# Splitting the second stream's blocks of normed tiles in halves of 512 columns

## The chip, the cores and the metric

One core of a Trainium2 chip runs the whole program: a two-layer network on 256 latent and 256 context tokens, in float32. The metric is the device time of one execution in microseconds (us). Engines are named as in the profile: PE is TensorE (matmul), DVE VectorE, ACT ScalarE, POOL GpSimd, SP SyncE; the last three also start DMAs.

## The reference, cut to what matters

```python
def _modulate(t, g, shift, scale):
    return _rms(t, g) * (1 + scale) + shift

def _swiglu(h, w13, w2):
    gte, up = jnp.split(h @ w13, 2, axis=-1)
    return (jax.nn.silu(gte) * up) @ w2

def _short_conv_mixer(h, w_in, k, w_out):
    bgate, cgate, xv = jnp.split(h @ w_in, 3, axis=-1)
    return (bgate * _dwconv3(cgate * xv, k)) @ w_out

# layer 0: FFN, conv mixer, FFN; layer 1: FFN, attention mixer, FFN; lat and cx are the two streams
lat = lat + 0.5 * mod[:, 0, 2] * _swiglu(_modulate(lat, norm_g[i, 0], ...), ffn_w13[i, 0], ffn_w2[i, 0])
cx = cx + 0.5 * modc[0, 2] * _swiglu(_modulate(cx, norm_g[i, 0], ...), ffn_w13[i, 0], ffn_w2[i, 0])
h = _modulate(lat, norm_g[i, 1], mod[:, 1, 0], mod[:, 1, 1])
hc = _modulate(cx, norm_g[i, 1], modc[1, 0], modc[1, 1])
...
```

The model width is 1024, the hidden width 2816. Every stage begins with the norm of the residual (RMS, scale, shift) of both streams, and then multiplies the normed tiles by that stage's first weights.

## The kernel before, in words

The residual `x` lies transposed, features on partitions: eight k tiles of 128 features, each 512 columns wide, columns 0 to 255 for the latent stream (s = 0) and 256 to 511 for the context stream (s = 1).

**Precision.** Each float32 operand is split in a rounded part and the rest (`split`: ACT copies the rounded part, L107; DVE subtracts it, L108). A product is then three matmuls (`mm3`): high by high (L136), the moving operand's low part (L137), the weights' low part (L138). So a matmul on L136 needs ACT's result alone, and one on L137 needs DVE's subtraction too. Names ending in h and l are such parts: `bh`, `bl` of the normed tiles, `wh`, `wl` of weights, `th`, `tl` of block sums.

**Blocks.** In three stages (the conv mixer, the second FFN of layer 0, the first FFN of layer 1) the normed tiles are kept as four blocks of 128 x 1024: features 0 to 511 or 512 to 1023, of stream 0 or 1. Each block holds four k tiles of 256 columns, as a float32 tile `hr` and as `bh`, `bl`. `Blocks.block` makes them: for each k tile, DVE scales x by the norm (`scaled`, L299, tile `t`, three buffers) and ACT adds the shift (L396, into `hr`). For stream 0 (`fine`) the two parts are made tile by tile (L391, L392). For stream 1 they are made once the four tiles of the block are there, by one `split` of 1024 columns.

**Openings.** The first work of such a stage is `opening`. PE multiplies two weight tiles by both streams, stream 0 first: 8 k tiles x 2 outputs (`pg`, `pu`) x 3 matmuls of 256 columns, for each weight tile. Under the second weight tile's products of stream 0 the norm of stream 1 is computed (`turn` in `tail_norm`), and then PE turns to stream 1. Meanwhile DVE and ACT build the sums of blocks T1 to T4 from the `hr` tiles (`sums`, L417 to L424).

**Pairs.** All further weights go through `Pair`, seven products of blocks in place of eight: `head` (A11 and A12), `five` (S1 by T1), `six` (S2 by T2, S4 by a block), `seven` (S3 by T3) and `four` (A22 by T4), accumulating in the PSUM tiles `p` and `q`. DVE forms the weights' sums (L731, L739), ACT and DVE split them, and DVE adds the halves of `q` and `sg` (L768).

**What sets the order.** Outside a few stretches that are ordered by hand, a scheduler places each engine's instructions in a queue, from its own estimate of when their inputs are there; each queue then runs in that order. So the code's order and the queue's differ, and a change of size moves instructions around it. Where a queue's next instruction waits, all behind it wait.

The function `tick(n)` places n pieces of the modulation vectors' work (DVE, L177) at its place in the code.

Of the kernel before, what the change touches and what calls it, by code (L numbers as in the profile page):

```python
# [20 lines left out]
T2 = 2 * S  # L21
# [27 lines left out]
def hybrid_kernel(ctx: ExitStack, tc: tile.TileContext, a: dict, out: bass.AP):  # L49
# [17 lines left out]
    def psum(s="ps"):  # L67
        return psm.tile([P, T2], F32, tag="mm", name=nm(s))
# [37 lines left out]
    def split(hi, lo, src):  # L106
        nc.scalar.activation(out=hi, in_=src, func=AF.Copy)  # L107
        return nc.vector.tensor_tensor(out=lo, in0=src, in1=hi.bitcast(F32), op=ALU.subtract)  # L108
# [80 lines left out]
    def streams(l, ch):  # L189
        return 1 if l == 1 and ch >= 5 else 2  # L190
# [9 lines left out]
    def next_unit():  # L200
        if not units:
            l, ch, pair, j = jobs.pop(0)
            mod_tile(l, ch)
            raw = coming.pop() if coming else load_mod(l, ch, pair, j)
            if jobs:
                coming.append(load_mod(*jobs[0]))
            units.extend((l, ch, pair, raw, j, v) for v in range(streams(l, ch)))
        if place:
            with tc.issue_after(place[0]):
                mod_unit(*units.pop(0))  # L210
        else:
            mod_unit(*units.pop(0))

    def tick(n, at=None):

        place[:] = [at] if at else []
        owed[0] += n
        while (jobs or units) and owed[0] >= 1:
            owed[0] -= 1
            next_unit()  # L220
        place.clear()
# [17 lines left out]
    def gate_of(l, j):  # L239

        ch = 3 * j + 2

        def get(m):
            while done.get((l, ch), 0) < (m // 2 + 1) * 2 * streams(l, ch):
                next_unit()
            return modv[l, ch]

        return get
# [66 lines left out]
    def hot(s, dt=F32R):  # L315
        return hop.tile([P, 1024], dt, name=nm(s), tag="hop")
# [56 lines left out]
    class Blocks:  # L373
# [5 lines left out]
        def block(self, s, hf, A, B, ri, fine=False, ks=range(4)):  # L379
            if ks[0] == 0:  # L380
                self.raw[hf, s] = hot("hr", F32)
                self.t["B", hf, s] = hot("bh"), hot("bl")
            raw = self.raw[hf, s]
            hi, lo = self.t["B", hf, s]
            for i in ks:
                k = 4 * hf + i
                c = slice(i * S, i * S + S)
                t = scaled(s, k, A, ri)
                b = B[:, k, s : s + 1]
                if fine:  # L390
                    nc.scalar.activation(out=hi[:, c], in_=t, func=AF.Identity, bias=b)  # L391
                    nc.vector.scalar_tensor_tensor(  # L392
                        out=lo[:, c], in0=t, scalar=b, in1=hi[:, c].bitcast(F32),
                        op0=ALU.add, op1=ALU.subtract,
                    )
                nc.scalar.activation(out=raw[:, c], in_=t, func=AF.Identity, bias=b)  # L396
            if not fine:
                split(hi, lo, raw)

        def at(self, k, c0, c1):  # L400
            return self.blk(("B", k // 4, c0 // S), k % 4)
# [411 lines left out]
    def ffn(l, b, h, tot, gate, tail, gs=(), ev=(0, 0), z=None):  # L813
        gs = list(gs)
        i0 = 0
        for t, n in enumerate(THIRDS):
            between = ()
            if tot == T2:
                heads = []
                if t == 0 and not gs:  # L820

                    gs = [new_pair("g") for _ in range(2)]
                    heads.append(opening(
                        h, [a["w13"][l, b, 0], a["w13"][l, b, 1], lambda: Pair(a["w13"][l, b, 2], h)],
                        lambda pp, i: w13_post(pp, gs[i], 0, T2),
                    ))
                prev = None
                for i in range(len(gs), n):
                    if t == 0 and not heads and i in AS_IS[l, b]:
                        w = load_w(a["w13"][l, b, i])  # L830
                        pp = psum("pg"), psum("pu")
                        if prev:
                            prev.seven()
                        if "T1" not in h.t:
                            with tc.issue_after(rows["W1"]):
                                h.sums()
                        w13_mm(pp, w, h, range(4), 0, T2)
                        if prev:
                            gs.append(new_pair("g"))
                            prev.four(gs[-1])  # L840
                            prev = None
                        w13_mm(pp, w, h, range(4, KT), 0, T2)
                        gs.append(new_pair("g"))
                        tick(3, w13_post(pp, gs[-1], 0, T2))
                        continue
                    if heads:
                        pr = heads.pop(0)
                    else:
                        pr = Pair(a["w13"][l, b, i0 + i], h)
                        pr.sums(0)  # L850
                        pr.sums(1)
                        pr.head()
                    pr.five()
                    at = prev.seven().ins if prev else None
                    pr.six()
                    if prev:
                        gs.append(new_pair("g"))
                        prev.four(gs[-1])
                    prev = pr
                    if i:  # L860
                        tick(0.9, at)

                def last():
                    gs.append(new_pair("g"))
                    prev.four(gs[-1])

                between = (prev.seven, last) if prev else ()
            else:
                for i in range(n):
                    w = load_w(a["w13"][l, b, i0 + i])  # L870
                    gs.append(beside(gp.tile([P, T2], F32R, name=nm("gx"), tag="gh")))
                    pp = psum("pg"), psum("pu")
                    if i0 + i < EARLY:
                        for k in range(KT):
                            for j in range(2):
                                ps = pp[j][:, : z.w]
                                mm3(ps, w(at13(1 - j, k)), z.at(k), k == 0, k == KT - 1)
                            if i == 0 and k == KT // 2:
                                flush(1)
                        if i < 3:  # L880
                            flush(1)
                        early_post(pp, gs[i], z.ri)
                        tick(1)
                        continue
                    for j in range(2):
                        ws = [w(at13(1 - j, k)) for k in range(KT)]
                        mm_wide(pp[j], ws, [h.both(k) for k in range(KT)], True, True)
                    beside_post(pp, gs[i])
                    tick(1)
            i0 += n  # L890

            def ws2(m):
                src = a["w2a"][l, b, m // 2] if t == 0 else a["w2b"][l, b, t - 1, m // 2]
                o = (m % 2) * n * P
                raw = load_raw(src[:, o : o + n * P], n * P)
                hi, lo = half()
                split(hi[:, : n * P], lo[:, : n * P], raw[:, : n * P])
                return lambda k: (hi[:, k * P : k * P + P], lo[:, k * P : k * P + P])

            cur = gs  # L900
            end = t == len(THIRDS) - 1
            project(
                ws2,
                (lambda k, c0, c1: cur[k]) if tot == S
                else lambda k, c0, c1: (cur[k][0][:, c0:c1], cur[k][1][:, c0:c1]), n,
                gate, tail if end else None, tot, 2 if end and tot == T2 else 0, ev[end], between,
            )
            gs = []


    h = Plain()
# [170 lines left out]
    ws, gs0, raws, cut = {}, [], {}, {}  # L1082
# [58 lines left out]
    h = FirstBlocks(h, h32)  # L1141
# [14 lines left out]


    hn = Blocks()
    ffn(0, 0, h, T2, gate_of(0, 0), tail_norm(0, 1, hn), gs0, (4, 3.4))
    h = hn  # L1160

    zs, ds = [], {}
# [52 lines left out]
    for n in range(2, len(parts)):  # L1215
# [8 lines left out]
        at = prev.seven().ins if prev else None  # L1224
# [22 lines left out]
    hn = Blocks()  # L1247
# [3 lines left out]
    )  # L1251
    h = hn
    hn = Blocks()
    ffn(0, 1, h, T2, gate_of(0, 2), tail_norm(1, 0, hn), (), (3.6, 3))
    h = hn


    hn = Plain()
    ffn(1, 0, h, T2, gate_of(1, 0), tail_norm(1, 1, hn), (), (2.8, 2.2))
    h = hn  # L1260
    ap = ctx.enter_context(tc.tile_pool(name="ap", bufs=2))

# [210 lines left out]
    aos, at, wos = [], [], {}  # L1473
    pieces = []
    for i in range(2):
        raw = [load_raw(a["wo"][i, :, c : c + 1024]) for c in (0, 1024)]
        hs = [half() for _ in range(2)]
        wos[i] = lambda o, hs=hs: tuple(t[:, o % 1024 : o % 1024 + P] for t in hs[o // 1024])
        for j in range(4):
            c = j % 2 * T2  # L1480
# [39 lines left out]
    hn, hz = Beside(), Early()  # L1520
# [89 lines left out]
```

## Time and profile before

| | |
|---|---|
| median of 3 runs | 1549.41 us (1548.96 to 1549.91) |
| the profiled execution | 1548.97 us, span 1547.2 us (1.8 us lie around the span) |
| granted TensorE clock | 1.00 |
| PE busy | 1533.5 us, 99% of the span |
| DVE, ACT, POOL busy | 1298.2, 852.2, 301.3 us |

A row of the timeline gives start and duration in us, engine, line, operation, output and inputs, shapes, count, and in brackets how long the engine was idle before it and what released it. Back-to-back instructions overlap in it, so what one costs its queue is the distance from its start to the next start. A matmul's end is modelled; how dense PE runs is read from starts. Line numbers are those of the kernel before; in the changed kernel all lines behind the edit stand one further.

### The profile page before, as it was taken

The page shows a single profiled execution, that of the slowest core. Times are in us where ns is not written, and L with a number is a line of the kernel's source. Part 1 is how long each engine was busy: PE and PEld are TensorE (multiplying, and loading weights), DVE is VectorE, ACT ScalarE, POOL GpSimd, SP SyncE. Part 2 cuts the span into 40 slices and gives each one's busy share as a digit, 9 for nine tenths or more (in the row PEclk, how much of TensorE's full clock was granted, in tenths as well). Part 3 has the DMA queues.
Part 4 walks back from the last instruction along what each step waited for, and adds up shares of the span by engine and source line. Part 5 has one row for each costly group of instructions (what it writes and reads, how often), then busy time and mean ns, then how long its engine had stood idle before and what let it go on. Part 6 is the DMA issues. An engine that isn't in the chain of part 4 may idle for free.

```text
span 1547.2 us, 27333 instructions
## 1 busy us (share of the span) xinstructions
PE 1533.5 (99%) x10594; PEld 1423.6 (92%) x10594; DVE 1298.2 (84%) x1964; ACT 852.2 (55%) x1468; POOL 301.3 (19%) x265
## 2 busy tenths in 40 slices
PE   8999999999999999999999999999999999999999
PEld 6898998999999899989999899989999899998888
DVE  5888788898989999968979889958968788998676
ACT  5644554645655376446456466446456456774553
POOL 0013313402231023042052112043042002300000
PEclk9999999999999999999999999999999999999999
DMA  9568768765356636695796625785697743476562
GB/s 377 199 188 235 162 184 232 164 194 143 75 143 175 206 91 151 212 216 135 213 214 153 207 68 136 220 189 138 210 220 182 253 159 114 142 246 220 170 195 76
DMA packets 97474, 278.80 MB, mean 180 GB/s; under 512 B 11456, under 2 KB 13120, under 8 KB 97344
## 3 DMA queue, kind: packets, MB, share of 16 engines
q1 hardware_dynamic: 69408, 228.10, 45.4%
q0 software_dynamic: 25920, 47.20, 18.1%
q10 hardware_dynamic: 2016, 1.76, 0.4%
q8 instruction: 83, 1.36, 0.4%
q14 instruction: 47, 0.39, 0.1%
HBM read 262.07 MB, written 1.05 MB: 170 GB/s over the span
## 4 chain that ended last, share of the span: by engine, by line
PE 89%; DVE 6%; DMA 2%; ACT 1%; issue 1%; POOL 0%; SPq 0%; DVEq 0%; POOLq 0%; ACTq 0%
PE p L138 8%; PE p L137 8%; PE p L136 8%; PE py L137 8%; PE py L136 8%; PE py L138 8%; PE q L138 6%; PE q L136 6%; PE q L137 6%; PE py L144 2%; PE pu L144 2%; PE pg L144 2%; DVE wl L108 1%; DMA wr<-in_w 1%; PE py L146 1%
## 5 line engine op out<-in xcount | busy, mean ns | idle before, releaser
L107 ACT ACTIVATE wh<-wr 128x1024 fp32r<-128x1024 f32 (+2 forms) x454 | 400.5, 909 | 289.2 <-PE py L137 94.5
L108 DVE TENSOR_TENSOR wl<-wr,wh 128x1024 fp32r<-128x1024 f32 (+2 forms) x454 | 468.6, 1056 | 107.0 <-ACT wh L107 87.0
L177 DVE CUSTOM_DVE_ANT_0 junk<-wr,scbc,first 128x1024 bf16<-128x1024 f32 x209 | 269.9, 1291 | 2.2 <-DMA wr<-in_modT 0.2
L137 PE MATMUL py<-gl,wh 128*128 128x512 f32 (+1 forms) x570 | 213.4, 374 | 0.0
L136 PE MATMUL py<-gh,wh 128*128 128x512 f32 (+1 forms) x570 | 213.4, 374 | 0.0
L138 PE MATMUL py<-gh,wl 128*128 128x512 f32 (+1 forms) x570 | 212.8, 373 | 0.0
L709 POOL TENSOR_SCALAR wr<-wr 128x512 f32<-128x512 f32 x66 | 125.4, 1900 | 424.0 <-DMA wr<-in_w 162.7
L136 PE MATMUL p<-th,wh 128*128 128x256 f32 x528 | 149.5, 283 | 0.0
L138 PE MATMUL p<-th,wl 128*128 128x256 f32 x528 | 149.4, 283 | 0.0
L137 PE MATMUL p<-tl,wh 128*128 128x256 f32 x528 | 149.4, 283 | 0.0
L138 PEld LDWEIGHTS py<-gh,wl 128*128 128x128 f32 x570 | 107.3, 188 | 19.1
L136 PEld LDWEIGHTS py<-gh,wh 128*128 128x128 f32 x570 | 107.4, 188 | 18.3
L137 PEld LDWEIGHTS py<-gl,wh 128*128 128x128 f32 x570 | 107.4, 188 | 18.2
L138 PE MATMUL q<-bh,wl 128*128 128x256 f32 x400 | 113.2, 283 | 0.0
L137 PE MATMUL q<-bl,wh 128*128 128x256 f32 x400 | 113.2, 283 | 0.0
L136 PE MATMUL q<-bh,wh 128*128 128x256 f32 x400 | 113.2, 283 | 0.0
L136 PEld LDWEIGHTS p<-th,wh 128*128 128x128 f32 x528 | 101.3, 192 | 0.4
L137 PEld LDWEIGHTS p<-tl,wh 128*128 128x128 f32 x528 | 101.3, 192 | 0.4
L138 PEld LDWEIGHTS p<-th,wl 128*128 128x128 f32 x528 | 101.3, 192 | 0.0
L114 POOL DMA_DIRECT2D w4l<-in_w x56 | 53.2, 949 | 229.9 <-ACT w4l L113 183.5
L566 POOL DMA_DIRECT2D x<-yg x48 | 44.7, 995 | 215.7 <-ACT yg L563 172.4
L772 ACT ACTIVATE sg<-sg 128x512 f32<-128x512 f32 x56 | 35.3, 631 | 89.0 <-DVE sg L768 88.9
(321 smaller groups left out, 4199.4 us busy)
## 6 DMA issues: line engine op xcount, KB each, us to landing
wr<-in_w SPq DMA_DIRECT2D x120, 512.0 KB, 4.8
wr<-in_modT SPq DMA_DIRECT2D x113, 512.0 KB, 5.1
wr<-in_w2b SPq DMA_DIRECT2D x64, 448.0 KB, 4.0
wr<-in_w2a SPq DMA_DIRECT2D x32, 512.0 KB, 4.4
wr<-in_w SPq DMA_DIRECT2D x56, 256.0 KB, 4.6
wr<-in_w POOLq DMA_DIRECT2D x56, 256.0 KB, 6.0
w4l<-in_w POOLq DMA_DIRECT2D x56, 256.0 KB, 5.8
x<-yg POOLq DMA_DIRECT2D x48, 256.0 KB, 7.6
```

The costliest lines, as they stand in the source:

```text
L107: nc.scalar.activation(out=hi, in_=src, func=AF.Copy)
L108: return nc.vector.tensor_tensor(out=lo, in0=src, in1=hi.bitcast(F32), op=ALU.subtract)
L114: nc.gpsimd.dma_start(out=lo, in_=src, accum_op=ALU.add)
L136: nc.tensor.matmul(ps, wh, mh, start=first, stop=False, **kw)
L137: nc.tensor.matmul(ps, wh, ml, start=False, stop=False, **kw)
L138: return nc.tensor.matmul(ps, wl, mh, start=False, stop=last, **kw).ins
L144: nc.tensor.matmul(ps, w[0], m[2], start=first and n == 0, stop=False)
L146: nc.tensor.matmul(ps[:, :S], w[1], m[0], start=False, stop=last and n == len(ms) - 1)
L177: nc.vector.tensor_tensor_reduce(out=junk, in0=raw, in1=scbc[:, v, :], scale=0.5 if ch in (2, 8) else 1.0, scalar=modb[:, l, col : col + 1 ...
L566: nc.gpsimd.dma_start(out=x[:, m, :], in_=t, accum_op=ALU.add)
L709: nc.gpsimd.tensor_scalar(out=r1[:, :T2], in0=r2[:, :T2], scalar1=-1.0, scalar2=None, op0=ALU.mult)
L772: nc.scalar.activation(out=self.sg, in_=self.sg, func=AF.Silu)
```

## The change

For stream 1 the `split` moves into the loop over the block's k tiles: behind the second and the fourth tile, of 512 columns each, in place of one of 1024 behind the fourth. `T2` is 512. In the three stages that is twelve splits in place of six, so six instructions more on ACT and six more on DVE. The literal 0.9 in `ffn` becomes the third number of a tuple that is 0.9 in each of the three calls that reach it, so that edit moves nothing.

```diff
@@ Blocks.block
                 nc.scalar.activation(out=raw[:, c], in_=t, func=AF.Identity, bias=b)
-            if not fine:
-                split(hi, lo, raw)
+                if not fine and i % 2:
+                    c = slice(c.stop - T2, c.stop)
+                    split(hi[:, c], lo[:, c], raw[:, c])
@@ ffn
-                        tick(0.9, at)
+                        tick(ev[2], at)
@@
-    ffn(0, 0, h, T2, gate_of(0, 0), tail_norm(0, 1, hn), gs0, (4, 3.4))
+    ffn(0, 0, h, T2, gate_of(0, 0), tail_norm(0, 1, hn), gs0, (4, 3.4, 0.9))
```

The scheduler's queues differ in three stretches, one behind each opening, and nowhere else on PE, DVE or ACT; POOL's and SP's are unchanged. In the rows below, a number behind a name tells tiles apart.

DVE's queue in the first opening (conv mixer), before. `t` is a scaled k tile of stream 1, `bl_4109` the low part of its first block, `bl_4126` of its second, L417 and L420 are sums of blocks in `hr`.

```order
L299 TENSOR_SCALAR t_4130<-x,A_3900,ss_4074 128x256
L299 TENSOR_SCALAR t_4133<-x,A_3900,ss_4074 128x256
L417 TENSOR_TENSOR hr_3922<-hr_4107,hr_3922 128x1024
L108 TENSOR_TENSOR bl_4109<-hr_4107,bh_4108 128x1024
L299 TENSOR_SCALAR t_4136<-x,A_3900,ss_4074 128x256
L420 TENSOR_TENSOR hr_4107<-hr_4124,hr_4107 128x1024
L108 TENSOR_TENSOR bl_4126<-hr_4124,bh_4125 128x1024
L108 TENSOR_TENSOR tl_4179<-hr_3922,th_4178 128x1024
```

The same place in the changed kernel (`bl_4109` the first block, `bl_4128` the second, whose two halves stand in one row as x2; L418 is the sum that was L417).

```order
L299 TENSOR_SCALAR t_4132<-x,A_3900,ss_4074 128x256
L108 TENSOR_TENSOR bl_4109<-hr_4107,bh_4108 128x512
L299 TENSOR_SCALAR t_4137<-x,A_3900,ss_4074 128x256
L299 TENSOR_SCALAR t_4140<-x,A_3900,ss_4074 128x256
L108 TENSOR_TENSOR bl_4109<-hr_4107,bh_4108 128x512
L418 TENSOR_TENSOR hr_3922<-hr_4107,hr_3922 128x1024
L108 TENSOR_TENSOR bl_4128<-hr_4126,bh_4127 128x512 x2
L108 TENSOR_TENSOR tl_4183<-hr_3922,th_4182 128x1024
```

Both halves of the first block's low part now stand ahead of the first sum of blocks, and the second sum (L420, now L421) has moved behind `tl`. The two FFN openings change in the same way.

DVE's queue at the second pair of the conv stage, before. `wl_4411` are the low parts of A11 and A12 of that pair, `sg_4317` needs PE's product `six` of the pair ahead, `wl_4418` are the low parts of its S1 and S2.

```order
L108 TENSOR_TENSOR wl_4411<-wr_4406,wh_4410 128x512
L108 TENSOR_TENSOR tl_4359<-hr_3971,th_4358 128x1024
L768 TENSOR_TENSOR sg_4317<-q_4316,sg_4317 128x512
L108 TENSOR_TENSOR wl_4411<-wr_4404,wh_4410 128x512
L731 TENSOR_TENSOR wr_4406<-wr_4406 128x512
L1207 TENSOR_TENSOR sg_4317<-xv_4230,sg_4317 128x512
L739 TENSOR_TENSOR wr_4404<-wr_4404,wr_4406 128x1024
L108 TENSOR_TENSOR wl_4418<-wr_4406,wh_4417 128x1024
```

The same place in the changed kernel, where these tiles are `wl_4415`, `sg_4321` and `wl_4422`.

```order
L108 TENSOR_TENSOR tl_4363<-hr_3971,th_4362 128x1024
L769 TENSOR_TENSOR sg_4321<-q_4320,sg_4321 128x512
L108 TENSOR_TENSOR wl_4415<-wr_4410,wh_4414 128x512
L108 TENSOR_TENSOR wl_4415<-wr_4408,wh_4414 128x512
L732 TENSOR_TENSOR wr_4410<-wr_4410 128x512
L777 TENSOR_TENSOR p_4319<-p_4319,gm_4378 128x256
L740 TENSOR_TENSOR wr_4408<-wr_4408,wr_4410 128x1024
L108 TENSOR_TENSOR wl_4422<-wr_4410,wh_4421 128x1024
```

The first half of A11 and A12's low parts has moved behind `tl` and the sum into `sg`; the addition to `p` (L776, now L777) has moved ahead of `wl_4422`, and L1207 behind it.

PE's queue where the second pair's S1 products begin (`q` by `th`), before: the first matmul on their low weights follows four matmuls behind the start.

```order
L136 MATMUL q_4432<-th_4178,wh_4417 128x256
L137 MATMUL q_4432<-tl_4179,wh_4417 128x256
L136 MATMUL p_4431<-th_4251,wh_4417 128x256
L137 MATMUL p_4431<-tl_4252,wh_4417 128x256
L138 MATMUL q_4432<-th_4178,wl_4418 128x256
```

The same place in the changed kernel, where `p_4319` by `w4h`, `w4l` is product `four` of the pair ahead.

```order
L137 MATMUL p_4435<-tl_4256,wh_4421 128x256
L136 MATMUL p_4319<-th_4362,w4h_4347 128x256
L137 MATMUL p_4319<-tl_4363,w4h_4347 128x256
L138 MATMUL p_4319<-th_4362,w4l_4348 128x256
L136 MATMUL p_4319<-th_4362,w4h_4347 128x256
L137 MATMUL p_4319<-tl_4363,w4h_4347 128x256
L138 MATMUL p_4319<-th_4362,w4l_4348 128x256
L136 MATMUL p_4319<-th_4362,w4h_4347 128x256
L137 MATMUL p_4319<-tl_4363,w4h_4347 128x256
L138 MATMUL p_4319<-th_4362,w4l_4348 128x256
L138 MATMUL q_4436<-th_4182,wl_4422 128x256
```

Nine of the twelve matmuls of the pair ahead's product `four` have moved in front of the first one that needs the low weights `wl_4422`.

More of the change, by code (lines that the diff above doesn't have):

```diff
@@ L1253, in hybrid_kernel @@
     hn = Blocks()
-    ffn(0, 1, h, T2, gate_of(0, 2), tail_norm(1, 0, hn), (), (3.6, 3))
+    ffn(0, 1, h, T2, gate_of(0, 2), tail_norm(1, 0, hn), (), (3.6, 3, 0.9))
     h = hn
     hn = Plain()
-    ffn(1, 0, h, T2, gate_of(1, 0), tail_norm(1, 1, hn), (), (2.8, 2.2))
+    ffn(1, 0, h, T2, gate_of(1, 0), tail_norm(1, 1, hn), (), (2.8, 2.2, 0.9))
     h = hn
```

## The prediction

> **What bounds the kernel now.** I read the page first, for the engine that sets the time, and where the chain of work runs.
>
> ```profile
> PE 1533.5 (99%) x10594; PEld 1423.6 (92%) x10594; DVE 1298.2 (84%) x1964; ACT 852.2 (55%) x1468; POOL 301.3 (19%) x265
> PE 89%; DVE 6%; DMA 2%; ACT 1%; issue 1%; POOL 0%; SPq 0%; DVEq 0%; POOLq 0%; ACTq 0%
> ```
>
> PE is the bound, and the change takes no matmul away. So it can only give back PE's gaps. The waits of PE name those that an opening can cause (total us, times, longest us):
>
> ```profile
> PE pg L136 <- ACT bh L391: 1.4, 1, 1.4
> PE pg L137 <- DVE bl L108: 1.2, 3, 0.4
> PE q L138 <- DVE wl L108: 1.0, 1, 1.0
> ```
>
> The second row is the tile that the change splits: three times, once in each opening. The first is of stream 0, and stays. The third will matter below. A wait's row counts idle time behind a matmul's modelled end; what PE loses is read from starts, in PE's timeline at the three places.
>
> ```profile
> 390.63 0.28 PE L136 MATMUL pg<-bh,wh 128*128 128x256 f32 x1
> 390.75 0.28 PE L136 MATMUL pu<-bh,wh 128*128 128x256 f32 x1
> 391.44 0.39 PE L137 MATMUL pg<-bl,wh 128*128 128x256 f32 x1 [0.41 <-DVE bl L108]
> ...
> 565.57 0.28 PE L136 MATMUL pu<-bh,wh 128*128 128x256 f32 x1
> 566.25 0.39 PE L137 MATMUL pg<-bl,wh 128*128 128x256 f32 x1 [0.40 <-DVE bl L108]
> ...
> 913.95 0.28 PE L136 MATMUL pu<-bh,wh 128*128 128x256 f32 x1
> 914.63 0.39 PE L137 MATMUL pg<-bl,wh 128*128 128x256 f32 x1 [0.40 <-DVE bl L108]
> ```
>
> A matmul of 256 columns starts 0.12 us behind the one ahead (390.63 to 390.75). The gap is 0.69 - 0.12 = 0.57, 0.68 - 0.12 = 0.56 and 0.56: 1.69 in all.
>
> Why it comes is in the timelines of DVE and ACT at the first opening.
>
> ```profile
> 386.28 2.83 DVE L299 SCALAR_TENSOR_TENSOR t<-x,A,ss 128x256 f32<-128x256 f32 x7 [0.67 <-PE ss L287]
> 389.03 1.22 DVE L417 TENSOR_TENSOR hr<-hr,hr 128x1024 f32<-128x1024 f32 x1
> 390.16 1.22 DVE L108 TENSOR_TENSOR bl<-hr,bh 128x1024 fp32r<-128x1024 f32 x1
> ...
> 392.35 1.22 DVE L420 TENSOR_TENSOR hr<-hr,hr 128x1024 f32<-128x1024 f32 x1 [0.58 <-ACT hr L396]
> 393.49 1.22 DVE L108 TENSOR_TENSOR bl<-hr,bh 128x1024 fp32r<-128x1024 f32 x1
> 394.63 1.22 DVE L108 TENSOR_TENSOR tl<-hr,th 128x1024 fp32r<-128x1024 f32 x1
> 395.76 1.29 DVE L108 TENSOR_TENSOR wl<-wr,wh 128x512 fp32r<-128x512 f32 x2
> ```
>
> ```profile
> 386.80 1.71 ACT L396 ACTIVATE hr<-t,mod 128x256 f32<-128x256 f32 x4 [2.51 <-DVE t L299]
> 388.54 1.06 ACT L107 ACTIVATE bh<-hr 128x1024 fp32r<-128x1024 f32 x1
> 389.51 1.29 ACT L396 ACTIVATE hr<-t,mod 128x256 f32<-128x256 f32 x3
> ...
> 394.26 1.14 ACT L107 ACTIVATE wh<-wr 128x512 fp32r<-128x512 f32 x2
> ```
>
> DVE has its tiles at 389.03, but ACT's `bh` ends at 389.60; the queue puts a block sum of 1.13 between, and `bl` ends at 391.38. PE was there at 390.87.
>
> **The change part by part.** *Prices.* A step on DVE costs its queue 1.13 for 1024 columns (390.16 less 389.03), 0.60 for 512 (two in 1.29, the last lasting 0.69), 0.39 for a `t` (2.75 / 7). On ACT it is 0.97 for 1024 (388.54 to 389.51), 0.53 for 512 (1.14 less 0.61), 0.40 for an `hr`. Two halves are dearer than a whole by 0.07 on DVE and 0.09 on ACT; with six blocks that is 0.4 and 0.5 us of work, on engines with idle time in most stages. What counts is when the first half ends.
>
> [...]
>
> *The opening, replayed with these prices in the new order.* ACT: `hr` at 386.80, 387.20, 387.60, the first half of `bh` at 388.00 to 388.62, `hr` at 388.53 and 388.93, the second half at 389.33 to 389.95. The second block's halves end at 391.28 and 392.21, T1's `th` at 393.17. DVE: six `t` to 388.64, first half of `bl` 388.66 to 389.35, two `t`, second half 390.00 to 390.69, the block sum to 391.74, the second block's two halves to 392.94, `tl` from 393.20, where it was 394.63. PE needs the first half of `bl` at 390.51 (two steps ahead of 390.75), the second twelve matmuls later at 391.8, the second block's from 393.4 and 394.8. All are there with 0.4 us or more to spare, so nothing takes the wait's place. The other openings show the same gap 174.81 and 523.19 us later (566.25 and 914.63 against 391.44) and have the same new order, so this holds there too: **-1.69** in all.
>
> *What it moves behind the opening.* In the conv stage PE's other wait lies 24 us further.
>
> ```profile
> 408.33 0.28 PE L136 MATMUL q<-bh,wh 128*128 128x256 f32 x1
> ...
> 414.72 0.28 PE L137 MATMUL p<-tl,wh 128*128 128x256 f32 x1
> 416.04 0.38 PE L138 MATMUL q<-th,wl 128*128 128x256 f32 x1 [1.05 <-DVE wl L108]
> ```
>
> ```profile
> 409.49 0.69 DVE L108 TENSOR_TENSOR wl<-wr,wh 128x512 fp32r<-128x512 f32 x1
> ...
> 411.23 0.69 DVE L768 TENSOR_TENSOR sg<-q,sg 128x512 f32<-128x512 f32 x1
> 411.83 0.69 DVE L108 TENSOR_TENSOR wl<-wr,wh 128x512 fp32r<-128x512 f32 x1
> ...
> 414.76 1.23 DVE L108 TENSOR_TENSOR wl<-wr,wh 128x1024 fp32r<-128x1024 f32 x1
> 415.90 0.43 DVE L776 TENSOR_TENSOR p<-p,gm 128x256 f32<-128x256 f32 x1
> ```
>
> PE loses 416.04 - 414.72 - 0.12 = 1.20 there. Both sides move. DVE: from `tl` (394.63) to the low weights of S1 is 20.13. New are the moved sum (+1.13) and the swap of L1207 for L776 (-0.60 + 0.33): they start at 393.20 + 20.99 = 414.19 and end at 415.42. PE passes 408.33 now at 407.76, and there is a new wait on the way: the first A11 low weights stood 14.86 behind `tl`, and now stand behind the moved sum, T4's `tl` (1.13) and the sum into `sg` (0.60) as well. They end at 393.20 + 14.86 + 2.86 + 0.69 = 411.61, while PE wants them 28 matmuls behind 407.76, at 411.12: **+0.50**. From there it is 33 matmuls (3.96), the moved nine of `four` among them, to the first on S1's low weights: 415.57, and they are there at 415.42. The wait of 1.20 goes: **-1.20**. The cover is 0.15, and each tenth by which DVE is later than that costs a tenth. What is queued behind the new place of `sg` on DVE are both halves of A11's and A12's low weights; only PE waits for them.
>
> *DMAs.* POOL's and SP's queues keep their order. Their starts follow DVE's releases, which come up to half a us earlier: nothing.
>
> *The sum.* -1.69 - 1.20 + 0.50 = -2.4 us. On the profiled execution's 1548.97 (span 1547.2 and 1.8 around it) that is 1546.6; this run lies 0.4 below the median, so on the median's scale it is 1549.41 - 2.4 = **1547.0**. About 0.2% (3.1 us) is what a measurement of this kernel can tell from no change; the sum is just inside it.
>
> **The rivals.** *DVE sets the pace behind the first opening (0.22).* The stretches:
>
> ```profile
> 392.00:420.00 28.00, 26.94 (x223) 26.53 (x222) 27.48 (x33) 17.80 (x28) 5.11 (x3) 1.00 0.25 67
> 420.00:450.00 30.00, 30.00 (x253) 30.00 (x252) 27.28 (x38) 18.17 (x31) 9.58 (x9) 1.00 0.53 123
> 515.00:547.00 32.00, 31.92 (x177) 27.82 (x175) 31.04 (x53) 12.66 (x19) 3.83 (x3) 1.00 0.58 187
> ```
>
> The third number behind the span is PE's, and so on to DVE's (27.48 of 28, 31.04 of 32). If DVE reaches S1's low weights no earlier than before, or if PE, earlier at the projection (515 to 547), waits longer for DVE there, the first opening's share is lost and only the other two stay: 1549.41 - 1.12 = 1548.3. For it speaks how full DVE is; against it that the 0.58 idle at 392.35 goes, and that DVE has 2.7 us idle from 420 to 450 in which it follows PE.
>
> *More comes off (0.20).* If the new wait of 0.50 does not come, since DVE catches up a few tenths, and the small gaps around 414 go too (PE's starts show 0.17 more there), it is -1.69 - 1.37 = -3.1 and, with what runs differ by, down to 1545.8: faster by over 0.2%.
>
> *Slower: ACT's copy in the two FFN openings (0.10).* PE may not add S2 by T2 onto `p` before ACT has copied `p` out (L756).
>
> ```profile
> 579.02 0.37 ACT L756 COPY sg<-p 128x256 f32<-128x256 f32 x1 [1.20 <-PE p L138]
> 579.29 0.64 ACT L107 ACTIVATE gh<-gm 128x512 fp32r<-128x512 f32 x1
> 579.98 1.06 ACT L107 ACTIVATE wh<-wr 128x1024 fp32r<-128x1024 f32 x1
> ```
>
> ```profile
> 581.58 0.28 PE L138 MATMUL q<-th,wl 128*128 128x256 f32 x1
> ...
> ACT wh L107 <- DVE wr L731: 67.7, 46, 3.6
> ```
>
> PE starts on `p` at 581.70 (581.58 and 0.12), so at 581.1 with the gap gone. In the new ACT queue the copy stands behind that `wh` and that `gh`, and `wh` waits for DVE's sum of weights (L739), which I replay to 577.8. Then the copy ends at 577.8 + 0.97 + 0.53 + 0.37 = 579.7 and 1.4 us cover it. If ACT stood there as long as its longest wait of this kind (3.6), PE would lose 2.2 in each of two openings: 1549.41 - 2.4 + 4.4 = 1551.4. It decides from a DVE 1.4 late, and turns the whole to a loss from 2.6. Against it: nothing ahead of that sum waits in DVE's rows.
>
> That the change does not do what it says can be ruled out from the queues: the halves stand where the replay has them.
>
> **How the numbers follow.** Forecast 0.48 (1546.4 to 1547.7), DVE's pace 0.22 (1548.3), more 0.20 (1545.8 to 1546.3), slower than before 0.10 (1551.4). The range takes the first three with 0.5 us for what runs differ by: 1545.7 to 1548.8. Faster by over 0.2% is below 1546.3: 0.22, the third case and the forecast's edge. Slower by over 0.2% is above 1552.5, where the ACT rival comes with a wait of 4.2 in both openings, or in one with more; since no row bounds that wait, I give it somewhat over half of that case: 0.06. The rest, 0.72, lies between.
>
> **What would show it.** The three waits of `pg` on L137 for `bl` are gone, and no wait for `bh` of L107 has come; six 1024-column rows of `bl` are twelve of 512 at 0.69. `tl` starts 1.4 us earlier in the openings. PE waits some 0.5 for `wl` at about 411 and not at 415. I am wrong if a wait of over 1 us for `wl` stands behind the first opening, if the projection's waits at 547 to 552 have grown, or if PE waits on L756 in the FFN openings.

## The result, and the profile after

The changed kernel takes 1546.49 us (median of 16 runs, 1545.01 to 1547.88); the kernel before took 1549.26 in as many runs beside it (1548.21 to 1551.24). The ratio is 0.9979, 95% interval 0.9972 to 0.9986: 2.8 us less, with 1.1 us of uncertainty to either side. The forecast was 2.4 less. The profiled execution took 1545.56 us with a span of 1543.8, at a clock of 1.0, against 1548.97 and 1547.2.

The page's busy times and the engines' shares of the chain, after:

```profile
PE 1532.5 (99%) x10594; PEld 1423.8 (92%) x10594; DVE 1299.2 (84%) x1970; ACT 850.3 (55%) x1474; POOL 301.3 (20%) x265
PE 93%; DVE 4%; ACT 1%; DMA 1%; issue 1%; POOL 0%; SPq 0%; DVEq 0%; ACTq 0%; POOLq 0%
```

PE has the same 10594 matmuls; DVE and ACT have six instructions more each. The chain runs through PE for 93% where it was 89%, and through DVE for 4% where it was 6%: waits have gone. Which ones, the waits of PE tell (total us, times, longest us); the two rows are those that answer to the three shown of before.

```profile
PE pg L136 <- ACT bh L391: 1.4, 1, 1.4
PE p L138 <- DVE wl L108: 0.6, 1, 0.6
```

`pg` on L137 for `bl` of L108 is gone, and so is `q` on L138 for `wl`. New is `p` on L138 for `wl`. (A wait of 0.4 for a `wl` at 1375.60, also in a tile called `pg`, is new too, but lies behind all three stages.) The place of each is in the timelines. DVE, ACT (one row) and PE (two rows) at the first opening, after:

```profile
387.90 0.69 DVE L108 TENSOR_TENSOR bl<-hr,bh 128x512 fp32r<-128x512 f32 x1
...
389.29 0.69 DVE L108 TENSOR_TENSOR bl<-hr,bh 128x512 fp32r<-128x512 f32 x1
389.89 1.22 DVE L418 TENSOR_TENSOR hr<-hr,hr 128x1024 f32<-128x1024 f32 x1
...
392.56 1.23 DVE L108 TENSOR_TENSOR tl<-hr,th 128x1024 fp32r<-128x1024 f32 x1 [0.24 <-ACT th L107]
```

```profile
391.48 1.05 ACT L107 ACTIVATE th<-hr 128x1024 fp32r<-128x1024 f32 x1
```

```profile
389.64 0.28 PE L136 MATMUL pg<-bh,wh 128*128 128x256 f32 x1
389.76 0.28 PE L137 MATMUL pg<-bl,wh 128*128 128x256 f32 x1
```

The first half of `bl` ends at 388.59 and PE uses it at 389.76, 0.12 behind the matmul ahead: no gap. This execution came to the opening 0.75 earlier than the other one (its norm's matmul L287 stands at 373.37 against 374.12), a difference that lies ahead of the first changed instruction and has nothing to do with the change. So 389.76 is 390.51 on the clock of before, where the prediction had it.

The second place, 20 us further, PE and then DVE:

```profile
410.18 0.28 PE L138 MATMUL p<-th,wl 128*128 128x256 f32 x1
411.03 0.39 PE L138 MATMUL p<-bh,wl 128*128 128x256 f32 x1 [0.58 <-DVE wl L108]
...
414.97 0.28 PE L138 MATMUL p<-th,w4l 128*128 128x256 f32 x1
415.09 0.28 PE L138 MATMUL q<-th,wl 128*128 128x256 f32 x1
```

```profile
407.43 2.36 DVE L108 TENSOR_TENSOR tl<-hr,th 128x1024 fp32r<-128x1024 f32 x2
409.69 0.69 DVE L769 TENSOR_TENSOR sg<-q,sg 128x512 f32<-128x512 f32 x1
410.30 1.29 DVE L108 TENSOR_TENSOR wl<-wr,wh 128x512 fp32r<-128x512 f32 x2
...
413.57 1.22 DVE L108 TENSOR_TENSOR wl<-wr,wh 128x1024 fp32r<-128x1024 f32 x1
```

The new wait costs 411.03 - 410.18 - 0.12 = 0.73. S1's low weights end at 414.79, and PE comes to them at 415.09 with no gap.

To sum up by stage I use the first matmul of each stage's norm of stream 0 (L287), from the timeline of PE; before, and then after:

```profile
374.12 0.71 PE L287 MATMUL ss<-first,ri 128*128 128x128 f32 x4
549.38 0.60 PE L287 MATMUL ss<-first,ri 128*128 128x128 f32 x4
897.38 0.71 PE L287 MATMUL ss<-first,ri 128*128 128x128 f32 x4
1245.98 0.71 PE L287 MATMUL ss<-first,ri 128*128 128x128 f32 x4
```

```profile
373.37 0.71 PE L287 MATMUL ss<-first,ri 128*128 128x128 f32 x4
546.74 0.60 PE L287 MATMUL ss<-first,ri 128*128 128x128 f32 x4
893.99 0.71 PE L287 MATMUL ss<-first,ri 128*128 128x128 f32 x4
1242.05 0.71 PE L287 MATMUL ss<-first,ri 128*128 128x128 f32 x4
```

The differences of neighbours are the lengths of the conv stage, of the second FFN of layer 0 and of the first FFN of layer 1. They leave out what lies ahead of the change and behind it, so they tell kernels apart better than medians do. They are not exact either: with whole blocks the conv stage is 175.26 and 174.74 long, and 0.40 of the difference is a wait at the projection that comes and goes (see the last section); the FFN of layer 0 is 348.00 to 348.25. The same rows of every run give this table, to which the experiments refer:

| run | conv | FFN, layer 0 | FFN, layer 1 | median minus the median of before beside it |
|---|---|---|---|---|
| before | 175.26 | 348.00 | 348.60 | |
| after | 173.37 | 347.25 | 348.06 | -2.77 |
| after, again | 173.59 | 347.28 | 348.04 | -2.36 |
| halves in the conv stage alone | 174.08 | 348.25 | 348.57 | -0.66 |
| halves in the FFNs alone | 174.74 | 347.27 | 348.05 | -1.84 |
| whole, block sum behind `bl` | 173.67 | 347.55 | 348.01 | -2.11 |
| second block halved alone | 173.63 | 348.14 | 348.52 | -2.01 |
| T4 later | 174.09 | 347.47 | 348.06 | -1.28 |
| taps later | 172.85 | 347.52 | 348.06 | -4.02 |
| taps later, again | 172.86 | 347.28 | 348.06 | -3.12 |
| whole, taps later | 173.54 | 348.19 | 348.57 | -1.21 |
| quarters | 173.38 | 347.71 | 348.16 | -1.37 |
| first `wh` held back | 172.69 | 348.89 | 348.08 | -1.39 |

An interval on a ratio reaches about 0.0009 to either side, 1.4 us, so the medians alone can't tell most of these variants apart. In the last row the border between the conv stage and the FFN lies elsewhere: behind the FFN's first row PE has 15 matmuls of the projection there and not 6, so 1.08 (nine of 0.12) belongs to the conv stage, which makes it 173.77 and 347.81. Gaps below are worked out from start to start, as in the prediction. In variants with added lines the line numbers stand a few further.

### The profile page after: what moved, and what is told of

Same layout as the page of the kernel before. It is cut to its first block, busy times and chain, and to the rows that moved or that the text cites. A ratio compares the mean times of both kernels' runs of the same rounds, so it can differ in the third digit from the quotient of the medians.

```text
span 1543.8 us, 27341 instructions
## 1 busy us (share of the span) xinstructions
PE 1532.5 (99%) x10594; PEld 1423.8 (92%) x10594; DVE 1299.2 (84%) x1970; ACT 850.3 (55%) x1474; POOL 301.3 (20%) x265
## 4 chain that ended last, share of the span: by engine, by line
PE 93%; DVE 4%; ACT 1%; DMA 1%; issue 1%; POOL 0%; SPq 0%; DVEq 0%; ACTq 0%; POOLq 0%
PE py L137 9%; PE py L136 9%; PE py L138 9%; PE p L138 8%; PE p L137 8%; PE p L136 8%; PE q L138 6%; PE q L136 6%; PE q L137 6%; PE py L144 2%; PE pu L144 2%; PE pg L144 2%; PE py L146 1%; DVE wl L108 1%; PE pg L146 1%; PE pu L146 1%
## 5 line engine op out<-in xcount | busy, mean ns | idle before, releaser
L108 DVE TENSOR_TENSOR wl<-wr,wh 128x1024 fp32r<-128x1024 f32 (+2 forms) x454 | 469.8, 1057 | 105.5 <-ACT wh L107 83.8
L137 PE MATMUL py<-gl,wh 128*128 128x512 f32 (+1 forms) x570 | 213.4, 374 | 0.0
L138 PE MATMUL py<-gh,wl 128*128 128x512 f32 (+1 forms) x570 | 212.8, 373 | 0.0
L137 PE MATMUL p<-tl,wh 128*128 128x256 f32 x528 | 149.4, 283 | 0.0
L138 PE MATMUL p<-th,wl 128*128 128x256 f32 x528 | 149.4, 283 | 0.0
L138 PEld LDWEIGHTS py<-gh,wl 128*128 128x128 f32 x570 | 107.3, 188 | 19.2
L137 PEld LDWEIGHTS py<-gl,wh 128*128 128x128 f32 x570 | 107.4, 189 | 18.0
L138 PE MATMUL q<-bh,wl 128*128 128x256 f32 x400 | 113.2, 283 | 0.0
L137 PE MATMUL q<-bl,wh 128*128 128x256 f32 x400 | 113.2, 283 | 0.0
L137 PEld LDWEIGHTS p<-tl,wh 128*128 128x128 f32 x528 | 101.3, 192 | 0.4
L138 PEld LDWEIGHTS p<-th,wl 128*128 128x128 f32 x528 | 101.3, 192 | 0.0
L740 DVE TENSOR_TENSOR wr<-wr,wr 128x1024 f32<-128x1024 f32 x66 | 81.5, 1235 | 1.8 <-ACT w4h L112 0.2
```

The lines of the kernel that those rows point to most:

```text
L137: nc.tensor.matmul(ps, wh, ml, start=False, stop=False, **kw)
L138: return nc.tensor.matmul(ps, wl, mh, start=False, stop=last, **kw).ins
L740: tt(out=v(r2), in0=v(r2), in1=s2.unsqueeze(1).to_broadcast([P, 2, T2]), op=ALU.subtract,)
```

## The experiments

**One part of the change at a time.** `Blocks` gets the number of k tiles behind which it splits: 2 in one kind of stage, 4 (as before) in the other.

```diff
-        def __init__(self):
-            self.raw, self.t = {}, {}
+        def __init__(self, n=2):
+            self.raw, self.t, self.n = {}, {}, n
...
-                if not fine and i % 2:
-                    c = slice(c.stop - T2, c.stop)
+                if not fine and (i + 1) % self.n == 0:
+                    c = slice(c.stop - self.n * S, c.stop)
```

Halves in the conv stage alone:

> Halves in the conv mixer's opening alone; the two FFN openings keep the whole split. If each opening's share stands by itself: the gap ahead of the first L137 of stream 1 is gone in the conv opening (0.57 to 0) and stays at 0.56 in both FFN openings; behind the conv opening PE waits some 0.7 us for low weights at about 411 and not 1.2 at 415; 1.3 to 1.9 us off, about 1547.5. If DVE sets the pace behind the conv opening: no more than 0.3 us off, about 1549.

PE's rows:

```profile
412.19 0.39 PE L138 MATMUL p<-bh,wl 128*128 128x256 f32 x1 [0.56 <-DVE wl L108]
...
565.72 0.39 PE L137 MATMUL pg<-bl,wh 128*128 128x256 f32 x1 [0.41 <-DVE bl L108]
...
914.10 0.39 PE L137 MATMUL pg<-bl,wh 128*128 128x256 f32 x1 [0.40 <-DVE bl L108]
```

Halves in the FFNs alone:

> Halves in the two FFN openings alone. If each opening's share stands by itself: 0.56 to 0.75 off in each, 1.1 to 1.5 in all, about 1548.0; the conv stage keeps its gap of 0.57 and its wait of 1.2 at 415, and PE keeps its 0.40 ahead of the sum of squares at the projection (546.6). If that 0.40 only differs from run to run, it may be gone here too, and be there in the run with halves in the conv opening alone.

```profile
391.18 0.39 PE L137 MATMUL pg<-bl,wh 128*128 128x256 f32 x1 [0.40 <-DVE bl L108]
...
415.79 0.39 PE L138 MATMUL q<-th,wl 128*128 128x256 f32 x1 [1.04 <-DVE wl L108]
```

Each opening's gap stays exactly where its block is whole, and the conv stage's two waits (0.56 at 391 and 1.2 at 415, or 0.72 at 412 in their place) go with the conv stage's halves. The medians were 1548.51 (ratio 0.9994, 0.9985 to 1.0003) and 1547.33 (0.9989, 0.998 to 0.9998); the two gains add up to 2.5, where the whole change gave 2.8 and 2.4, but the first one's interval does not tell it from nothing. By the table the FFN of layer 1 gives 0.52 and the one of layer 0 0.7 to 1.0; the conv stage was 174.74 and 175.26 long whole, and 173.37 to 174.08 in halves: on the average 1.3 less.

**The order alone.** The splits stay whole, and the first block sum is held behind the `bl` of the first block in DVE's queue.

```diff
             if not fine:
-                split(hi, lo, raw)
+                self.cut[hf] = split(hi, lo, raw).ins
...
-        h.sums(0)
+        with tc.issue_after(h.cut[0]):
+            h.sums(0)
```

> Whole splits as before, but the first sum of blocks pinned behind the first block's low part on DVE, in all three openings. If the order in DVE's queue is the cause: bl starts when ACT's bh ends (389.66 in place of 390.16) and the gap goes from 0.57 to 0.1; the scheduler then gives the same new order behind the opening as with halves, so the wait at 415 goes and one of 0.7 comes at 411; 2.0 to 2.5 off, about 1547.0, nearly all that the halves bring. If the halves' size is the cause (a part must end sooner): gaps of 0.4 or more stay, for the first or the second block, and at most 1 us comes off.

DVE at the first opening, and PE:

```profile
390.20 1.23 DVE L108 TENSOR_TENSOR bl<-hr,bh 128x1024 fp32r<-128x1024 f32 x1 [0.52 <-ACT bh L107]
...
391.73 1.22 DVE L417 TENSOR_TENSOR hr<-hr,hr 128x1024 f32<-128x1024 f32 x1
...
415.08 1.22 DVE L108 TENSOR_TENSOR wl<-wr,wh 128x1024 fp32r<-128x1024 f32 x1
```

```profile
412.55 0.39 PE L138 MATMUL p<-bh,wl 128*128 128x256 f32 x1 [0.65 <-DVE wl L108]
```

None of the three gaps is left, though `bl` is as large as before and DVE even idles 0.52 for it; the FFNs are as long as with halves (347.55, 348.01), and the wait at 412 has come as well (0.81). Median 1547.06, ratio 0.9987 (0.9978 to 0.9995). The gap was a matter of what stands in DVE's queue ahead of `bl`, and not of its size; the halves do nothing for PE in the openings that this does not. (Halves with the sum kept ahead of the first block's `bl` were not run.) Behind the opening, T1's `tl` starts later here than before, 21.24 us after the stage's first row (374.69) and not 20.51. S1's low weights (the row at 415.08) still end earlier, after 41.61 and not 41.87, and PE has the nine matmuls of `four` ahead of them, as in the changed kernel.

**The second block alone.** The first block stays whole with the sum ahead of its `bl`, so the gaps should stay; DVE's idle time behind them goes.

```diff
-                if not fine and i % 2:
-                    c = slice(c.stop - T2, c.stop)
+                n = 2 if hf else 4
+                if not fine and (i + 1) % n == 0:
+                    c = slice(c.stop - n * S, c.stop)
```

> Halves for the second block (features 512 to 1023) alone, the first block's split whole and behind the sum as before. The three gaps of 0.57 stay. If what lies behind the conv opening is a matter of queue order and of DVE's idle 0.58 there: that idle time goes, the wait of 1.2 at 415 goes and at most 0.3 comes at 411, so 1.0 to 1.5 off, about 1548.0. If the gain behind the opening comes from the opening's gap alone: no change, 1549.3.

PE:

```profile
391.12 0.39 PE L137 MATMUL pg<-bl,wh 128*128 128x256 f32 x1 [0.40 <-DVE bl L108]
...
411.25 0.28 PE L138 MATMUL p<-th,wl 128*128 128x256 f32 x1
411.51 0.38 PE L138 MATMUL p<-bh,wl 128*128 128x256 f32 x1
```

The gap is there (and in both FFNs, whose lengths are those of before), and yet the conv stage takes 173.63, as with halves. At 411 PE now loses 0.14 and not 0.73. So the 0.57 that the halves give back in the conv opening is taken again at 411. What the conv stage gains shows at S1's low weights. They end 41.45 us after the stage's first row (41.42 in the changed kernel, 41.87 before), so 0.4 earlier, and PE does nine matmuls of `four` (1.08) ahead of them that stood behind them before. My estimate from the rows of before: DVE's 0.45 alone would leave 0.75 of the wait of 1.20, and the nine matmuls alone 0.07, since PE would come at 414.72 + 0.12 + 1.08 = 415.92 to weights that end at 415.99. So PE's own order is the larger part; no run moves these nine matmuls alone. Median 1547.16, ratio 0.9988 (0.9979 to 0.9997).

**Is DVE the pace from the opening to S1?** Two kernels move work around that stretch. In the first, T4's split is done later, in the code behind the second pair's first sums of weights.

```diff
-                keep("T4", b21)
+                if n == 2:
+                    keep("T4", b21)
+                else:
+                    self.late = lambda: keep("T4", b21)
...
             pr.sums(0)
+            if n == 3:
+                h.late()
             pr.sums(1)
```

> The changed kernel, but in the conv stage the split of T4 stands in the code behind the second pair's first sums of weights, no longer behind the first pair's. On DVE that takes T4's `tl` (1.14) and the sum into `sg` from ahead of the first low weights of A11, where PE waited 0.73, and puts `tl` ahead of the low weights of S1; the nine matmuls of `four` that PE had ahead of those go behind them. Theory (behind the conv opening DVE sets PE's pace, and the wait stands wherever its queue is furthest behind): the wait at 411 goes (-0.7), but S1's low weights are ready at 415.0 while PE, without those nine matmuls, wants them at 413.2 to 413.5; a wait of 1.5 to 1.8 comes, the conv stage is some 1.0 longer than in the changed kernel, and the median about 1547.5. Rival (it is only the order at this one place): -0.7, 1545.8.

PE:

```profile
413.98 0.28 PE L137 MATMUL p<-tl,wh 128*128 128x256 f32 x1
415.32 0.39 PE L138 MATMUL q<-th,wl 128*128 128x256 f32 x1 [1.07 <-DVE wl L108]
```

The wait at 411 is gone, and one of 1.22 stands at S1's low weights (415.32 - 413.98 - 0.12). From the stage's first row (374.19) PE has come 41.13 us to them, with nine matmuls of `four` (1.08) still to do that the changed kernel has behind it there: 42.21, against 415.09 - 373.37 = 41.72. That is 0.5 later, half of the 1.0 expected, and the rival's gain did not come. (The length of the whole stage doesn't show it: one run with halves was as long.) Median 1547.91, ratio 0.9985 (0.9977 to 0.9994). In the second, the work that leaves the stretch is some that nobody waits for there: the two shifted additions of the first conv tile.

```diff
+        def shifts():
             ...
+        if m:
+            shifts()
+        else:
+            late.append(shifts)
...
             pr.sums(0)
+            if n == 3:
+                with tc.issue_after(pr.cut):
+                    late.pop()()
             pr.sums(1)
```

> The changed kernel, but the two shifted additions of the first conv tile (L1173 and L1177 of m = 0, 0.66 each on DVE) are done behind the low weights of the second pair's S1 and not among the block sums. Theory (DVE sets the pace from the opening to those weights): 1.32 of work that nobody waits for leaves that stretch, the wait of 0.73 at 411 goes and S1's low weights are ready at 413.3 where PE wants them at 413.2; the conv stage is some 0.7 shorter than in the changed kernel, median about 1545.8. Rival (PE is the pace and 0.73 is a local accident): the wait moves elsewhere or the time stays within 0.2 of 1546.5.

DVE, and PE at the places of the two waits:

```profile
411.45 1.22 DVE L108 TENSOR_TENSOR wl<-wr,wh 128x1024 fp32r<-128x1024 f32 x1
```

```profile
408.52 0.28 PE L138 MATMUL p<-th,wl 128*128 128x256 f32 x1
408.64 0.28 PE L138 MATMUL p<-bh,wl 128*128 128x256 f32 x1
...
412.52 0.28 PE L137 MATMUL p<-tl,wh 128*128 128x256 f32 x1
412.73 0.38 PE L138 MATMUL q<-th,wl 128*128 128x256 f32 x1
```

Both waits are gone (0.09 is left at 412.73, where the low weights end at 412.67), and the stage takes 172.85. From its first row (372.81) to S1's low weights PE needs 39.92, with the same nine matmuls to come 41.00: 0.72 less than in the changed kernel, just the wait. Median 1545.17 in 6 runs, ratio 0.9970 (0.9958 to 0.9981). As this lay further below than 0.7, I ran the kernel once more, beside the changed kernel:

> The changed kernel with the taps moved, once more, on one chip with the changed kernel. Theory: conv stage 0.5 to 0.7 shorter than in the changed kernel, and the median below it by as much. Rival: the 1.3 by which the first run's median lay lower was what runs differ by, and nothing is left.

> The changed kernel as it is, for the comparison with the taps moved. Both theories: 1546.5, within what its runs differ by (1545.0 to 1547.9), the wait at 411 of 0.7 in its profile and no gap ahead of the first `bl`.

They gave 1545.68 (ratio 0.9982, 0.9973 to 0.9991) and 1546.44 (0.9984, 0.9975 to 0.9993), and conv stages of 172.86 and 173.59: 0.73 less, which is the wait. The kernel with the taps moved is the fastest of those run. The medians differ by 0.76, but the two intervals overlap by far, and the changed kernel's conv stage was 173.37 the first time. What carries the reading is the way from the stage's first row to S1's low weights, with the nine matmuls counted in: 41.72 in both runs of the changed kernel and 41.00 in both with the taps moved.

Then the same move without the change, on whole splits, with the diff above applied to the kernel before:

> The kernel before (whole splits of 1024), with the two shifted additions of the first conv tile behind the second pair's S1 low weights, as in the run with the taps moved. Theory (two causes that add: the order in the opening costs PE 0.56 three times, and DVE's queue behind the conv opening costs it 1.2 to 1.4 at S1): the three gaps ahead of the first `bl` stay, the wait of 1.20 for S1's low weights goes, the conv stage is some 1.3 shorter, the median is 1.3 below the kernel before, about 1547.9. Rival (without the load on DVE the splits' size matters nowhere): the three gaps go too, and it comes out with the changed kernel plus taps at about 1545.2.

```profile
393.40 0.38 PE L137 MATMUL pg<-bl,wh 128*128 128x256 f32 x1 [0.40 <-DVE bl L108]
...
416.33 0.28 PE L136 MATMUL p<-th,wh 128*128 128x256 f32 x1
416.45 0.35 PE L138 MATMUL q<-th,wl 128*128 128x256 f32 x1
```

The three gaps stay, the wait of 1.20 goes, the conv stage is 173.54 long (1.2 to 1.7 less), and the FFNs are those of before. Median 1547.59, ratio 0.9994 (0.9986 to 1.0003). S1's low weights end 40.27 us after the stage's first row here, 1.6 earlier than before, and the nine matmuls of `four` stand behind them as before. So there are two causes, the queue's order in the openings and DVE's lateness behind the conv opening. A lighter DVE removes the second; in the changed kernel most of it is covered by PE's new order instead. In the conv stage the second covers the first until the load goes, and then halving brings another 0.4 by S1's low weights (41.00 against 41.44) and 0.7 by the stage's end; the rest I did not follow.

**The price of a split.** The changed kernel with a split behind each k tile.

```diff
-                if not fine and i % 2:
-                    c = slice(c.stop - T2, c.stop)
+                if not fine:
                     split(hi[:, c], lo[:, c], raw[:, c])
```

> The changed kernel with four splits of 256 columns for each block of stream 1 in place of two of 512: twelve more instructions on DVE and on ACT in the three openings. It measures what an added split costs DVE's queue. [...]

DVE, the first block, and PE in the FFN of layer 0:

```profile
389.49 0.76 DVE L108 TENSOR_TENSOR bl<-hr,bh 128x256 fp32r<-128x256 f32 x2
390.16 0.47 DVE L299 SCALAR_TENSOR_TENSOR t<-x,A,ss 128x256 f32<-128x256 f32 x1
```

```profile
588.58 0.39 PE L138 MATMUL q<-th,wl 128*128 128x256 f32 x1 [0.18 <-DVE wl L108]
```

Two quarters cost DVE's queue 390.16 - 389.49 = 0.67, so a block 1.34, against 1.20 in halves: 0.07 for each added instruction, which is also what two halves cost more than a whole in the rows of before (1.20 against 1.13). At that price I took the wait at 411 to grow by some 0.3, four of 0.07 in the opening, and the median to be about 1546.8. The openings have no gap, but the wait at 411 is not longer (0.75 against 0.73 in halves); a wait of 0.33 is new at S1's low weights in the FFN of layer 0, and both FFNs are longer than with halves (347.71 and 348.16). Median 1547.82, ratio 0.9989 (0.9981 to 0.9998): quarters give nothing that halves don't.

**The wait that the change left.** PE's longest wait in an opening, 1.59 in the FFN of layer 0, is for `bh`, behind a `wh` on ACT. That `wh` is held behind it.

```diff
+            if c >= 1024 and behind:
+                with tc.issue_after(behind):
+                    split(hi[:, d], lo[:, d], raw[c // 1024][:, d])
...
-        w = [load_w(srcs[0])]
+        w = [load_w(srcs[0], behind=pin and h.first)]
```

> The changed kernel, but in the opening of the second FFN of layer 0 the split of the first weights' second half is held behind the first `bh` of stream 0. There PE waited 1.59 for that `bh`, which stood on ACT behind this `wh` (547.98 to 548.94); the change left that wait as it was. Theory (this wait is ACT's queue and lies beside the change): `bh` can start at about 547.95, so some 1.0 of the 1.59 goes and the median is about 1545.5. Rival: the low weights that follow on DVE come too late for the fifth k tile, PE waits there instead, and the time stays at 1546.5 or above.

PE in that opening:

```profile
549.20 0.28 PE L140 MATMUL pg<-bh,wh 128*128 128x256 f32 x1
...
550.74 0.38 PE L140 MATMUL pg<-bh,wh 128*128 128x256 f32 x1 [0.37 <-ACT bh L395]
...
552.79 0.39 PE L141 MATMUL pg<-bl,wh 128*128 128x256 f32 x1 [0.55 <-DVE bl L397]
```

No wait stands ahead of the first `pg` at 549.20, and four smaller ones stand behind it (0.19, 0.53, 0.17 and 0.71, together 1.60): what was saved was given back within 4 us, while the next tiles' `bh` and `bl` still come one by one. The three stages together are 0.8 to 1.0 longer than in the two runs of the changed kernel. Median 1547.80, ratio 0.9989 (0.9980 to 0.9998). My theory for it fell. But the edit moved more than the `wh`: nine matmuls of the projection now stand behind the FFN's first row, ahead of the first `pg`, so the run does not show what the `wh` alone costs there.

## Why the prediction was right

- **The three gaps, -1.69.** Right in kind and size at the place, in all three openings; the order run shows the queue as the cause. In the FFNs they reach the end of the stage: 0.54 and 0.75 in the two profiled executions (0.56 each forecast; the rest of the 0.75 lies in gaps of under 0.2 that I did not follow). In the conv stage the gap is given back at 411, which the sum held as +0.50 against -0.57.
- **The new wait, +0.50.** It came, 0.73. The term was 0.23 too small. On the clock of before (0.75 added), ACT's `th` of T1 ends at 393.28 and not at 393.17, so `tl` starts at 393.31 and not at 393.20, 1.3 earlier than before and not 1.4, and A11's low weights end at 411.74 and not at 411.61. PE wanted them at 411.05 and not at 411.12. That is 0.69; the wait by starts is 0.73.
- **The wait of 1.20 goes.** It did, and the 0.17 ahead of it. S1's low weights ended at 415.54 on the clock of before against a forecast of 415.42. That is only 0.45 earlier than before (415.99), and 0.27 of it is the swap of L1207 for L776. The rest of the 1.20 PE fills with the nine matmuls of `four`, which the forecast had among its 33. Of the cover of 0.15 no more than 0.03 would have been left, but PE came at 415.84, later by the longer wait.
- **The sum.** -0.57 + 0.50 - 1.20 = -1.27 for the conv stage, measured -1.3 as the mean of three runs with the changed conv stage against the mean of two without; -1.12 for the FFNs, measured -1.3 by the table. The places named here add up to -1.69 + 0.73 - 1.37 = -2.33 in the rows: 0.23 too little for the new wait and 0.17 too little for what went nearly cancel, which is luck. The medians' 2.8, with 1.1 of uncertainty, could not tell -2.4 from 1 us more or less. Between the two profiled executions the spans differ by 3.4: 0.75 lie ahead of the change, 3.2 in the three stages, and 0.5 are given back behind them.
- **The rival of DVE's pace** was right that DVE sets the pace from the opening to S1 (the runs with the second block alone and with the taps moved). Its condition, low weights of S1 no earlier than before, was nearly met. `tl` is 1.3 earlier, but the second block sum (1.13) only moved behind `tl` and still stands ahead of those weights, so they come 0.45 earlier. What it left out is PE's queue. With the nine matmuls counted in, PE passes S1's low weights 41.92 + 1.08 = 43.00 us after the stage's first row before and 41.72 after: 1.28 less, of which DVE's 0.45 is the smaller part.
- **More comes off** was not the case: its condition was that the new wait stays away, and in the changed kernel it came. With the taps moved it does stay away.
- **ACT's copy** cost nothing. In the FFN of layer 0, after:

```profile
575.43 1.06 ACT L107 ACTIVATE wh<-wr 128x1024 fp32r<-128x1024 f32 x1 [0.91 <-DVE wr L740]
...
576.92 0.35 ACT L757 COPY sg<-p 128x256 f32<-128x256 f32 x1
```

The `wh` waits 0.91 for DVE's sum and not up to 3.6, the copy is out at 577.27, 1.1 ahead of PE's first use of `p` at 578.41 (forecast 1.4), and no wait of PE on L757 stands in the profile.

- **Prices.** Twelve `bl` of 512 took 686 ns each, 0.60 in the queue, as taken. Two slips in the working change nothing: in the rows of stretches the first number behind the length is PE's and the third DVE's, as the figures for DVE are then used; and the second half of `bl` is needed at 390.51 + 12 x 0.12 = 391.95, not at 391.8.

## What to carry to other kernels

When a bound engine waits for a small step, look at what stands ahead of that step in its producer's queue before cutting the step: moving a block sum behind `bl` did about as much as halving `bl` (2.1 us off against 2.4 and 2.8 by the medians). Here a gap taken out upstream was worth only what the next producer that set the pace let through: the conv opening's 0.57 was taken again at 411, while the two FFNs, with gaps of 0.56, became 0.54 and 0.75 shorter. So replay the queue to the place where its lead is smallest and put both the gap and the new wait in the sum. Look at the bound engine's own order too: nine matmuls moved ahead of the late weights covered 1.08 of a wait of 1.20 by their starts, though no run moves them alone. And compare stages by their own start and end rows: what lies ahead of the change can differ between two executions by as much as the whole effect (the conv stage starts between 372.81 and 376.09 here). Check first that the same instructions stand on either side of those rows.

## What the runs showed of the hardware that was not expected

Ahead of the first opening PE runs the same instructions in the same order in all these kernels, at a granted clock of 0.999 to 1.0, and still their executions do not come to it at the same time; single executions of the changed kernel itself lie between 1544.85 and 1547.88. PE's waits in the first FFN, in runs of three kernels (before, quarters, and after again):

```profile
272.76 0.38 PE L136 MATMUL q<-hh,wh 128*128 128x256 f32 x1 [1.25 <-ACT gm L762]
```

```profile
274.00 0.39 PE L136 MATMUL q<-hh,wh 128*128 128x256 f32 x1 [1.65 <-ACT gm L762]
```

```profile
104.28 0.39 PE L138 MATMUL q<-th,wl 128*128 128x256 f32 x1 [0.52 <-DVE wl L108]
```

The first wait is 1.25 in one run and 1.65 in another, and the last is not there in the run of before at all. The start of the conv stage lay between 372.81 and 376.09 in thirteen profiles. The same holds for a wait of 0.40 at the projection (546.64 to 547.16 in the kernel before), which was gone in the run with halves in the FFNs alone, whose conv stage is unchanged. Why these waits differ from one execution to the next was not tried and stays open.
